# Memory keys as fp32 matmuls, and the input x loaded and normalised earlier, in a hybrid decoder step

## The chip, the cores and the metric

One core of a Trainium2 chip runs the whole program once. The metric is the device time of one execution in microseconds (us); the number to predict is the median of the changed kernel's runs.

## What is computed

One step of a decoder layer for 1024 prompt tokens and 8 sample tokens, 1032 columns together, width 1024. What matters here is its beginning: keys and values of 256 memory tokens, and the norm of x with which every later product starts.

```
def rms_norm(x, g):
    y = xf * rsqrt(mean(xf * xf, axis=-1) + EPS)
    return y * g

def memory_kv(mem, g, w_mk, w_mv):
    m = rms_norm(mem, g)
    k = einsum('bmd,de->bme', m, w_mk)     # 256 x 1024 by 1024 x 1024
    v = einsum('bmd,de->bme', m, w_mv)
...
h = rms_norm(x, g_mix)
z = einsum('btd,de->bte', h, w_in)         # the first product over x: the indexer's keys
```

All arrays are fp32. Behind this come a short convolution, a sparse attention whose keys are picked by an indexer, attention to the memory, a gated feed-forward block and a last norm.

## The kernel before, in words

Everything lies with its features on partitions: x is eight tiles of 128 features by 1032 columns (`xs`), the memory two tiles of 128 by 1024, each with four pieces of 128 features by 256 memory tokens (`memr`). Weights come as units of 128 x 1024 (512 KB), each eight blocks of 128 x 128; `weight_plan` fixes their order. Units 0 to 7 are the memory keys' weights (one for each group of 128 outputs), 8 to 15 the memory values', unit 16 is called "ikdup" (the weight of the indexer's keys, twice side by side), 17 and 18 the indexer's queries, 19 and 20 the attention keys.

To keep fp32 accuracy, a product is made of three matmuls on rounded operands (type fp32r): high by high, high by low, low by high. The high part of a tile is a ScalarE copy to fp32r, the low part the difference to the original, on VectorE or GpSimd. `Weights.split_to` (lines 156 to 169) does that for weights: L164 the high part, L166 the low part, on the engines of `lo_engines` in turn. `take` (L171) loads weights up to `ahead` units further, splits up to `sahead` units and hands out eight blocks. `split_sb` (L491) does it for tiles of x, with the gain folded in when it has a scale (L493, L498).

A hand-made order decides everything: each engine works its instructions in the order of the program text, and the tiles are taken from a ring of 49 slots (`Slots`). All the loads here are issued on SyncE's queue in text order, stores among them being issued at the next `flush`.

At the start (lines 370 to 396) the queue gets the gains, memory and unit 0 in halves, and then units 1 to 8 in turn with the eight tiles of x, then units 9 and 10 and small tensors. Lines 670 to 685 split the memory (scaled by its gain) and unit 0.

The key loop (lines 715 to 747) has eight steps of 24 matmuls of 256 columns (L726). Beside them run the squares of memory (L720), their sums and the row sum (`rstd_sum`, `rstd_chain`, `rstd_rows`: ones-matmuls at L436 and L455, small VectorE steps, copies at L456), squares of x (L697, ScalarE) and their running sum (L703, VectorE), and the evictions (L708), which multiply by the memory's norm. Units 1 to 7 get their low parts on GpSimd and VectorE in turn.

The value loop (lines 758 to 794) has eight steps of 12 matmuls of 512 columns (L770). After step 2 comes the row sum of x's squares, after step 3 the norm's rows (`xR`) and the first two normalisations; `xnorm` (L752, 753) multiplies a tile of x by `xR`, on VectorE for even tiles and on GpSimd for odd ones; from step 4 on a step has one `xnorm` and one `xsplit` (split with the gain); the rest follow the loop. Then `lo_engines` is GpSimd alone.

Next come "ikdup" (`dense`, L809: 72 matmuls of 344 columns at L474, tile k of x wanted by the k-th nine of them), the copies of its result (L503, L506, L812), and `x_sums` (L538), which multiplies two raw tiles of x by the gain on ScalarE (L541) and makes sums and differences of halves on VectorE for the later product units (`unit`, L584, matmuls at L603); it is called four times, in lines 816 to 923. The second attention-key product is copied out by L915, behind the last `x_sums`.

Of the kernel before, what the change touches and what calls it, by code (L numbers as in the profile page):

```python
# [16 lines left out]
T = 1032  # L17
# [13 lines left out]
X_AFTER = (2, 3, 4, 5, 6, 7, 8, 9)  # L31
X_SQUARE = (1, 2, 3, 4, 5, 6, 7, 8)
# [103 lines left out]
class Weights:  # L136
# [19 lines left out]
    def split_to(self, n):  # L156
# [3 lines left out]
        while self.split < n:  # L160
# [8 lines left out]
            self.split += 1  # L169

# [149 lines left out]
def build(tc, A):  # L320
# [56 lines left out]
    def load_x():  # L377
        if len(xs) < 8:
            xs.append(S.get())
            nc.sync.dma_start(xs[-1][0][:, :T], A["xT"][len(xs) - 1])  # L380

    wraw = S.get()
    for hf in range(2):
        c = slice(512 * hf, 512 * hf + 512)
        load_mem(0, hf)
        nc.sync.dma_start(wraw[0][:, c], A["ws"][0][:, c])
    W.loaded = 1
    load_mem(1, 0)
    load_mem(1, 1)
    for n in X_AFTER:  # L390
        W.load_to(n)
        load_x()
# [145 lines left out]
    def x_sums(hl, gi, p, xa, xb):  # L538

        for x, o in ((xa, 2 * p), (xb, 2 * p + 1)):  # L540
            ACT.activation(x[0][:, :T], x[0][:, :T], AF.Copy, scale=gain(gi, o))  # L541
# [128 lines left out]
    mh, ml = [S.get(F32R), S.get(F32R)], [S.get(F32R), S.get(F32R)]  # L670
    msq = [S.get(), S.get()]
    W.lo_engines = [G, V]
    wh, wl = S.get(F32R), S.get(F32R)
    for k in range(8):
        a, c = k // 4, (k % 4) * 256
        ACT.activation(mh[a][0][:, c:c + 256], memr[a][0][:, c:c + 256], AF.Copy, scale=gain(GKV, k))
        V.scalar_tensor_tensor(ml[a][0][:, c:c + 256], memr[a][0][:, c:c + 256], gain(GKV, k),
                               mh[a][0].bitcast(F32)[:, c:c + 256], op0=ALU.mult, op1=ALU.subtract)
        if k in (1, 3):
            c = slice(256 * (k - 1), 256 * (k - 1) + 512)  # L680
            ACT.activation(wh[0][:, c], wraw[0][:, c], AF.Copy)
            V.tensor_tensor(wl[0][:, c], wraw[0][:, c], wh[0].bitcast(F32)[:, c], op=ALU.subtract)
    S.put(wraw)
    W.H[0], W.L[0] = wh, wl
    W.split = 1
# [6 lines left out]
    xR = [None]  # L692
# [21 lines left out]
    dgm = None  # L714
    for j in range(8):
        blocks = W.take(8)
# [17 lines left out]
        if j == 2:  # L734
# [4 lines left out]
        if j == 3:  # L739
            rstd_rows(dgm, 128, mR[0], 256, 256)  # L740
        if j in X_SQUARE:
            x_square(X_SQUARE.index(j))
        if j - 1 in X_SQUARE:
            x_accum(X_SQUARE.index(j - 1))
        if j >= 3:
            for q in ([0, 1, 2, 3] if j == 3 else [j]):
                evict_mk(q)
    S.put(mR)
    dgx = None
    h = []  # L750

    def xnorm(k):  # L752
        (V if k % 2 == 0 else G).tensor_tensor(xs[k][0][:, :T], xs[k][0][:, :T], xR[0][:, :T], op=ALU.mult)

    def xsplit(k):
        h.append(split_sb(xs[k], scale=gain(GMIX, k)))

    for hv in range(2):
        for kp in range(4):
# [14 lines left out]
            j = 8 + step  # L774
            if j in X_SQUARE:
                x_square(X_SQUARE.index(j))
            if j - 1 in X_SQUARE:
                x_accum(X_SQUARE.index(j - 1))
            if step == 2:
                rstd_sum(xacc[0][0], 86, 12)  # L780
                dgx = rstd_chain(86, 12)
                S.put(xacc[0])
                xR = S.get()
            if step == 3:
# [1385 lines left out]
```

## Time and profile before

| what | value |
| --- | --- |
| median of 3 runs | 2087.91 us (2087.48 to 2088.03) |
| time of the profiled execution | 2086.61 us |
| its span in the profile | 2084.8 us |
| busy: TensorE matmuls / weight loads | 2037.8 / 1974.7 us |
| busy: VectorE / ScalarE / GpSimd | 1250.9 / 837.6 / 449.8 us |

The span runs from the first to the last instruction; the time of the execution has some 1.8 us around it. Engines: PE is TensorE's matmul, PEld its weight load, which overlaps PE, DVE is VectorE, ACT ScalarE, POOL GpSimd, SPq SyncE's queue. L166 is line 166 of the kernel. In the chain of waits that ended last, TensorE's two main matmul lines, L603 and L474, stand first with 19% and 15% of the span. Matmuls are pipelined: the recorded duration of one (some 280 ns for 256 columns) is longer than the distance to the next, so rates are read from distances between starts.

### The profile page before, as it was taken

What the parts mean: (1) busy time and instruction counts of PE and PEld (TensorE: products, weight loads), DVE (VectorE), ACT (ScalarE), POOL (GpSimd) and SP (SyncE); (2) the same over time, 40 slices, a digit from 0 to 9 for tenths busy, and PEclk for the clock granted to TensorE, in tenths of its full rate; (3) what the DMA queues carried; (4) which work ended last, traced back from release to release, by engine and by line L of the source; (5) the groups of instructions that cost most, each with busy time, mean ns of one, the idle gap of its engine ahead of it and who ended that gap; (6) DMA issues with size and microseconds to landing.
All of it is one profiled execution on the core that took longest, in us unless ns stands there. A gap on an engine that the chain in (4) does not pass through costs nothing. (4 is left out here: it accounts for less than half of the span.)

```text
span 2084.8 us, 35217 instructions
## 1 busy us (share of the span) xinstructions
PE 2037.8 (98%) x14519; PEld 1974.7 (95%) x14519; DVE 1250.9 (60%) x2169; ACT 837.6 (40%) x1345; POOL 449.8 (22%) x323
## 2 busy tenths in 40 slices
PE   8899999999999999999999999999999999999998
PEld 7799999999999996889999989999999999999997
DVE  7856667788866446861234787467677677721114
ACT  5547767675333334751122252343222222322203
POOL 3410000000000232324424442420000000174404
PEclk9999999999999999999999999999999999999999
DMA  7212221212335531052424424211221321453102
GB/s 295 87 41 82 87 77 62 82 59 65 127 109 214 213 130 54 1 193 92 133 82 152 174 111 163 102 51 58 95 82 62 102 82 62 156 200 102 51 1 82
DMA packets 79874, 217.49 MB, mean 104 GB/s; under 512 B 9690, under 2 KB 24354, under 8 KB 79714
## 3 DMA queue, kind: packets, MB, share of 16 engines
q1 hardware_dynamic: 79170, 214.73, 29.7%
q8 instruction: 113, 1.85, 0.4%
q10 hardware_dynamic: 544, 0.53, 0.1%
q14 instruction: 47, 0.39, 0.1%
HBM read 167.28 MB, written 47.94 MB: 103 GB/s over the span
## 5 line engine op out<-in xcount | busy, mean ns | idle before, releaser
L603 PE MATMUL PS<-t,t 128*128 128x258 f32 x7392 | 894.8, 284 | 7.7 <-DVE t L1893 3.2
L603 PEld LDWEIGHTS PS<-t,t 128*128 128x128 f32 x7392 | 891.6, 190 | 10.8 <-DVE t L1893 3.4
L474 PE MATMUL PS<-t,t 128*128 128x344 f32 x4824 | 770.7, 321 | 2.8 <-POOL t L166 1.2
L474 PEld LDWEIGHTS PS<-t,t 128*128 128x128 f32 x4824 | 762.5, 189 | 6.8 <-POOL t L166 1.8
L166 POOL TENSOR_TENSOR t<-t,t 128x1024 fp32r<-128x1024 f32 x78 | 196.5, 2526 | 415.3 <-ACT t L164 212.1
L246 DVE TENSOR_TENSOR t<-t,t 128x1024 fp32r<-128x1024 f32 (+1 forms) x176 | 188.8, 1086 | 6.4 <-ACT t L233 6.4
L233 ACT ACTIVATE t<-t 128x1024 fp32r<-128x1024 f32 (+1 forms) x176 | 161.6, 946 | 70.6 <-DVE t L223 60.7
L955 ACT ACTIVATE PS<-t,cand 128x1024 f32<-128x1024 f32 (+4 forms) x160 | 143.8, 899 | 54.4 <-DVE cand L962 51.5
L525 POOL TENSOR_TENSOR t<-t,t 128x1032 fp32r<-128x1032 f32 x22 | 53.6, 2453 | 416.6 <-ACT t L524 402.1
L1973 DVE TENSOR_TENSOR t<-PS,t 128x1032 f32<-128x1032 f32 x32 | 39.5, 1233 | 163.0 <-PE PS L474 163.0
L164 ACT ACTIVATE t<-t 128x1024 fp32r<-128x1024 f32 x86 | 89.7, 1050 | 76.0 <-PE PS L474 60.4
L655 DVE TENSOR_TENSOR t<-t,t 128x1032 f32<-128x1032 f32 (+1 forms) x100 | 114.1, 1149 | 2.8 <-ACT t L1879 2.3
L609 DVE TENSOR_TENSOR t<-PS,t 128x516 f32<-128x516 f32 x44 | 30.6, 695 | 109.2 <-PE PS L603 109.2
L607 ACT COPY t<-PS 128x516 f32<-128x516 f32 x44 | 25.9, 588 | 166.4 <-PE PS L603 166.1
L1534 DVE TENSOR_TENSOR t<-PS,t 128x1032 f32<-128x1032 f32 x32 | 39.4, 1232 | 79.9 <-PE PS L474 79.9
L1605 DVE CUSTOM_DVE_ANT_0 caus<-t,t 128x256 bf16<-128x256 f32 x128 | 79.0, 617 | 10.0 <-ACT t L1647 5.2
L493 ACT ACTIVATE t<-t 128x1032 fp32r<-128x1032 f32 (+2 forms) x24 | 25.5, 1068 | 132.9 <-DVE t L1517 76.9
L496 POOL TENSOR_TENSOR t<-t,t 128x1032 fp32r<-128x1032 f32 (+1 forms) x22 | 53.5, 2438 | 109.1 <-ACT t L493 91.3
L1094 POOL COPY co<-cst 128x8 f32<-128x8 f32 x8 | 1.5, 192 | 340.4 <-DVE cst L1089 340.4
L1226 POOL TENSOR_SCALAR t<-t,ast 128x128 f32<-128x128 f32 (+7 forms) x64 | 47.8, 747 | 120.4 <-DVE ast L1225 84.6
L612 ACT COPY t<-PS 128x516 f32<-128x516 f32 x26 | 15.3, 590 | 144.8 <-PE PS L603 144.8
L524 ACT ACTIVATE t<-t 128x1032 fp32r<-128x1032 f32 x40 | 41.4, 1059 | 74.9 <-PE PS L474 44.9
(272 smaller groups left out, 2108.6 us busy)
## 6 DMA issues: line engine op xcount, KB each, us to landing
t<-in_ws_dram SPq DMA_DIRECT2D x86, 512.0 KB, 5.2
t<-in_wu_dram SPq DMA_DIRECT2D x44, 512.0 KB, 4.3
t<-in_wu_dram SPq DMA_DIRECT2D x88, 256.0 KB, 5.5
fd<-t SPq DMA_DIRECT2D x18, 516.0 KB
t<-fd SPq DMA_DIRECT2D x18, 516.0 KB, 10.1
t<-in_xT_dram SPq DMA_DIRECT2D x16, 516.0 KB, 7.1
t<-in_cmk_dram SPq DMA_DIRECT2D x16, 512.0 KB, 5.9
t<-in_cmv_dram SPq DMA_DIRECT2D x16, 512.0 KB, 5.4
```

Of the source, the lines that this page charges most:

```text
L164: nc.scalar.activation(h[0][:, :1024], raw[0][:, :1024], AF.Copy)
L166: eng.tensor_tensor(l[0][:, :1024], raw[0][:, :1024], h[0].bitcast(F32)[:, :1024], op=ALU.subtract)
L233: self.nc.scalar.activation(h[0][:, :w], self.raw[u][x][0][:, :w], AF.Copy)
L246: self.nc.vector.tensor_tensor(l[0][:, o:o + w], raw[0][:, :w], h[0].bitcast(F32)[:, :w], op=ALU.subtract)
L474: PE.matmul(PS[:, b + c, :CH], w, x[0][:, c * CH:(c + 1) * CH], start=(k == 0 and p == 0), stop=(k == n - 1 and p == 2))
L496: (lo or G).tensor_tensor(l[0][:, :width], src[0][:, :width], hf, op=ALU.subtract)
L525: lo.tensor_tensor(l[0][:, a:b], raw[0][:, a:b], h[0].bitcast(F32)[:, a:b], op=ALU.subtract)
L603: PE.matmul(PS[:, banks[z] + c, :HC], a, b[:, HC * c:HC * c + HC], start=j < 3 and q == 0 and p == 0 or j == 5 and q == 0 and p == 0, stop ...
L655: V.tensor_tensor(o, o, i, op=ALU.mult)
L955: ACT.activation(wide[:, :128 * (i + 1)], sc[i], AF.Sign, bias=candf[:, n:n + 1], scale=-1.0, accum_out=tval[:, n:n + 1])
L1226: G.tensor_scalar(p, p, a[:, 3:4], 1.0, op0=ALU.mult, op1=ALU.mult)
L1605: V.tensor_tensor_reduce(out=caus, in0=s[0][:, 256 * x:256 * x + 256], in1=rows, scale=1.0, scalar=0.0, op0=ALU.mult, op1=ALU.add, accum_o ...
```

## The change

The memory keys are computed with one fp32 matmul for each block in place of three fp32r matmuls. Their weights are used as loaded (`take_raw`), without a split; the memory, multiplied by its gain, is one tile pair `mg`, made by ScalarE and VectorE in turn, and is split only at step 2, for the values. x is loaded two tiles at a time between units 2 and 6, squared in steps 1 to 5 of the keys, and its row sums come behind step 6, its norm's rows behind step 7. In the value loop each step has one `xnorm`, now with the gain in it and on VectorE, and one `xsplit` with its low part on VectorE. Since x then holds the gain, `x_sums` leaves out its ScalarE passes in its four calls. The weights' low parts are on VectorE up to unit 20, and on GpSimd again from `begin_conv_out` on.

```
-X_AFTER = (2, 3, 4, 5, 6, 7, 8, 9)
-X_SQUARE = (1, 2, 3, 4, 5, 6, 7, 8)
+X_SQUARE = {1: (0,), 2: (1,), 3: (2, 3), 4: (4, 5), 5: (6, 7)}
...
+    def take_raw(self):
+
+        self.load_to(self.cur + 1 + self.ahead)
+        self.cur += 1
+        return self.raw.pop(self.cur - 1)
+
...
-    W.loaded = 1
+        nc.sync.dma_start(w0[0][:, c], A["ws"][0][:, c])
+    W.loaded, W.split = 1, 8
     load_mem(1, 0)
     load_mem(1, 1)
-    for n in X_AFTER:
-        W.load_to(n)
-        load_x()
+    for w, x in ((3, 2), (4, 4), (5, 6), (6, 8)):
+        W.load_to(w)
+        load_x(x)
     W.load_to(11)
...
-        for x, o in ((xa, 2 * p), (xb, 2 * p + 1)):
-            ACT.activation(x[0][:, :T], x[0][:, :T], AF.Copy, scale=gain(gi, o))
+        if gi is not None:
+            for x, o in ((xa, 2 * p), (xb, 2 * p + 1)):
+                ACT.activation(x[0][:, :T], x[0][:, :T], AF.Copy, scale=gain(gi, o))
...
-    W.lo_engines = [G, V]
-    wh, wl = S.get(F32R), S.get(F32R)
+    mg = [S.get(), S.get()]
+    W.lo_engines = [V]
     for k in range(8):
         a, c = k // 4, (k % 4) * 256
...
+        o, i = mg[a][0][:, c:c + 256], memr[a][0][:, c:c + 256]
+        if k % 2 == 0:
+            ACT.activation(o, i, AF.Copy, scale=gain(GKV, k))
+        else:
+            V.tensor_scalar(o, i, gain(GKV, k), None, op0=ALU.mult)
...
+    def xnorm(k):
+        V.scalar_tensor_tensor(xs[k][0][:, :T], xs[k][0][:, :T], gain(GMIX, k), xR[0][:, :T], op0=ALU.mult, op1=ALU.mult)
+
+    def xsplit(k):
+        h.append(split_sb(xs[k], lo=V))
+
     for j in range(8):
-        blocks = W.take(8)
+        w = W.take_raw()
         flush()
...
-        order = [(p, k) for k in range(8) for p in range(3)] if j == 0 else [(p, k) for p in range(3) for k in range(8)]
-        for p, k in order:
+        for k in range(8):
             a, c = k // 4, (k % 4) * 256
-            w, x = ((0, mh), (0, ml), (1, mh))[p]
-            PE.matmul(PS[:, j % 6, :256], blocks[k][w], x[a][0][:, c:c + 256], start=(k == 0 and p == 0),
-                      stop=(k == 7 and p == 2))
-        W.close()
+            PE.matmul(PS[:, j % 6, :256], w[0][:, 128 * k:128 * k + 128], mg[a][0][:, c:c + 256], start=k == 0, stop=k == 7)
+        S.put(w)
...
-        if j == 2:
+        if j == 1:
             rstd_sum(msq[0][0], 128, 2)
...
-        if j == 3:
+        if j == 2:
             rstd_rows(dgm, 128, mR[0], 256, 256)
...
+            for a in range(2):
+                hl = split_sb(mg[a], lo=V, width=1024)
+                mh.append(hl[0])
+                ml.append(hl[1])
+        for k in X_SQUARE.get(j, ()):
+            x_square(k)
+        for k in X_SQUARE.get(j - 1, ()):
+            x_accum(k)
+        if j >= 2:
+            for q in ([0, 1, 2] if j == 2 else [j]):
                 evict_mk(q)
+        if j == 6:
+            rstd_sum(xacc[0][0], 86, 12)
+            dgx = rstd_chain(86, 12)
+            S.put(xacc[0])
+            xR = S.get()
+            W.split_to(9)
+        if j == 7:
+            rstd_rows(dgx, 86, xR[0], T, CH)
...
             step = 4 * hv + kp
...
+            xnorm(step)
+            if step >= 1:
+                xsplit(step - 1)
...
-    W.lo_engines = [G]
-    for k in range(4, 8):
-        if k < 6:
-            xnorm(k + 2)
-        xsplit(k)
+    xsplit(7)
...
     def begin_conv_out():
+        W.lo_engines = [G]
```

## Rows read from the trace of the kernel before

**Rows 1.** The page, part 1: busy time, share of span, instructions of each engine

```profile
PE 2037.8 (98%) x14519; PEld 1974.7 (95%) x14519; DVE 1250.9 (60%) x2169; ACT 837.6 (40%) x1345; POOL 449.8 (22%) x323
```

**Rows 2.** Busy time by stretches: width, PE, PEld, DVE, ACT, POOL, granted clock, DMA

```profile
6.00:11.00 5.00, 4.62 (x17) 3.99 (x18) 4.02 (x9) 3.74 (x9) 0.00 (x0) 1.00 0.96 365
...
63.00:70.00 7.00, 0.00 (x0) 0.00 (x0) 7.00 (x3) 0.65 (x1) 7.00 (x3) 0.72 0.04 17
70.00:76.00 6.00, 5.81 (x18) 5.43 (x19) 6.00 (x5) 3.47 (x4) 2.39 (x1) 0.50 0.24 90
```

**Rows 3.** Waits of PE from 0 to 190 us: total, times, longest

```profile
PE PS L770 <- DVE t L166: 8.2, 2, 7.5
...
PE PS L603 <- ACT t L915: 2.5, 1, 2.5
...
PE PS L474 <- POOL t L166: 1.0, 1, 1.0
```

**Rows 4.** Groups by line and shape, 46 to 72 us: busy, mean ns, idle before

```profile
L753 POOL TENSOR_TENSOR t<-t,t 128x1032 f32<-128x1032 f32 x4 | 13.6, 3411 | 0.8 <-ACT t L793 0.8
...
L166 DVE TENSOR_TENSOR t<-t,t 128x1024 fp32r<-128x1024 f32 x2 | 6.8, 3414 | 0.0
```

**Rows 5.** Timeline of DVE and ACT, 40 to 86 us: start, duration of the group

```profile
40.70 2.56 DVE L703 TENSOR_TENSOR t<-t,t 128x1032 f32<-128x1032 f32 x2
...
42.02 1.23 DVE L703 TENSOR_TENSOR t<-t,t 128x1032 f32<-128x1032 f32 x1
...
73.40 2.49 DVE L498 SCALAR_TENSOR_TENSOR t<-t,gains,t 128x1032 fp32r<-128x1032 f32 x2
75.81 1.22 DVE L753 TENSOR_TENSOR t<-t,t 128x1032 f32<-128x1032 f32 x1
...
85.64 1.03 ACT L503 ACTIVATE t<-PS 128x1032 fp32r<-128x1032 f32 x1 [5.42 <-PE PS L474]
```

**Rows 6.** Timeline of PE: fp32r streams of 256, 512 and 344 columns

```profile
28.88 7.17 PE L726 MATMUL PS<-t,t 128*128 128x256 f32 x56 [1.81 <-DVE t L166]
35.89 8.92 PE L770 MATMUL PS<-t,t 128*128 128x512 f32 x36
...
163.22 11.55 PE L474 MATMUL PS<-t,t 128*128 128x344 f32 x72
```

**Rows 7.** Timeline of PE and PEld around fp32 matmuls, L1037 and L2030

```profile
618.42 3.65 PE L1037 MATMUL PS<-t,t 64*32 64x257 f32 x16
...
622.00 0.22 PE L1038 MATMUL PS<-iwc,sel 8*32 8x4 f32 x2
...
2051.79 0.19 PEld L1993 LDWEIGHTS PS<-t,t 128*128 128x128 f32 x1 [0.17 <-issue]
2052.15 0.98 PEld L1993 LDWEIGHTS PS<-t,t 128*128 128x128 f32 x6 [0.17 <-issue]
```

**Rows 8.** Groups of PE, 6.3 to 11 and 12 to 16 us; timeline, first instructions

```profile
L726 PE MATMUL PS<-t,t 128*128 128x256 f32 x17 | 4.9, 456 | 3.9 <-ACT t L681 3.9
...
L726 PE MATMUL PS<-t,t 128*128 128x256 f32 x37 | 4.5, 280 | 0.0
...
6.38 10.56 PE L726 MATMUL PS<-t,t 128*128 128x256 f32 x64 [3.90 <-ACT t L681]
...
10.61 1.06 ACT L164 ACTIVATE t<-t 128x1024 fp32r<-128x1024 f32 x1 [0.16 <-DMA t<-in_ws_dram]
...
15.75 1.06 ACT L164 ACTIVATE t<-t 128x1024 fp32r<-128x1024 f32 x1 [0.28 <-DMA t<-in_ws_dram]
```

**Rows 9.** Timeline: row sums of x's squares, rows of the norm, VectorE's last copy

```profile
44.65 1.93 PE L436 MATMUL PS<-ones,t 128*86 128x1 f32 x24
...
49.31 2.20 PE L455 MATMUL PS<-t,ones 86*128 86x344 f32 x6
...
51.55 0.52 DVE L456 COPY t<-PS 128x344 f32<-128x344 f32 x1 [0.94 <-PE PS L455]
```

**Rows 10.** Timeline: the low part of unit 18 on POOL

```profile
96.10 2.68 POOL L166 TENSOR_TENSOR t<-t,t 128x1024 fp32r<-128x1024 f32 x1 [13.21 <-ACT t L164]
```

More of the change, by code (lines that the diff above doesn't have):

```diff
@@ L375, in load_mem, with load_x @@
         nc.sync.dma_start(memr[a][0][:, c], A["memT"][:, 4 * a + 2 * hf:4 * a + 2 * hf + 2, :].rearrange("p k m -> p (k m)"))
-    def load_x():
-        if len(xs) < 8:
+    def load_x(n):
+        while len(xs) < n:
             xs.append(S.get())
             nc.sync.dma_start(xs[-1][0][:, :T], A["xT"][len(xs) - 1])
-    wraw = S.get()
+    w0 = S.get()
+    W.raw[0] = w0
     for hf in range(2):
@@ L385, in build @@
         load_mem(0, hf)
-        nc.sync.dma_start(wraw[0][:, c], A["ws"][0][:, c])
-    W.loaded = 1
+        nc.sync.dma_start(w0[0][:, c], A["ws"][0][:, c])
+    W.loaded, W.split = 1, 8
     load_mem(1, 0)
     load_mem(1, 1)
-    for n in X_AFTER:
-        W.load_to(n)
-        load_x()
+    for w, x in ((3, 2), (4, 4), (5, 6), (6, 8)):
+        W.load_to(w)
+        load_x(x)
     W.load_to(11)
@@ L668, in join @@
         return out
-    mh, ml = [S.get(F32R), S.get(F32R)], [S.get(F32R), S.get(F32R)]
     msq = [S.get(), S.get()]
-    W.lo_engines = [G, V]
-    wh, wl = S.get(F32R), S.get(F32R)
+    mg = [S.get(), S.get()]
+    W.lo_engines = [V]
     for k in range(8):
         a, c = k // 4, (k % 4) * 256
[L676 to L685, printed above, removed]
+        o, i = mg[a][0][:, c:c + 256], memr[a][0][:, c:c + 256]
[3 more added lines that the diff above has]
+            V.tensor_scalar(o, i, gain(GKV, k), None, op0=ALU.mult)
     mR = S.get()
@@ L691, in build @@
     xacc = [None]
-    xR = [None]
     xsq = [None] * 8
@@ L712, in evict_mk @@
                   mstage[a][0][:, :1024].rearrange("p (k m) -> p k m", m=256), mstage[a])
-    dgm = None
+    dgm = dgx = None
+    mh, ml = [], []
+    h = []
+    def xnorm(k):
+        V.scalar_tensor_tensor(xs[k][0][:, :T], xs[k][0][:, :T], gain(GMIX, k), xR[0][:, :T], op0=ALU.mult, op1=ALU.mult)
+    def xsplit(k):
+        h.append(split_sb(xs[k], lo=V))
     for j in range(8):
-        blocks = W.take(8)
+        w = W.take_raw()
         flush()
@@ L738, in build @@
             S.put(msq[0])
-        if j == 3:
+        if j == 2:
             rstd_rows(dgm, 128, mR[0], 256, 256)
[L741 to L746, printed above, removed]
-                evict_mk(q)
-    S.put(mR)
[L749 to L756, printed above, removed]
+            for a in range(2):
[8 more added lines that the diff above has]
+            for q in ([0, 1, 2] if j == 2 else [j]):
+                evict_mk(q)
+        if j == 6:
[6 more added lines that the diff above has]
+            rstd_rows(dgx, 86, xR[0], T, CH)
+    for t in mg:
+        S.put(t)
+    S.put(mR)
     for hv in range(2):
@@ L773, in build @@
             step = 4 * hv + kp
[L774 to L784, printed above, removed]
-                rstd_rows(dgx, 86, xR[0], T, CH)
-                xnorm(0)
-                xnorm(1)
-            if step >= 4:
-                xnorm(step - 2)
-                xsplit(step - 4)
+            xnorm(step)
+            if step >= 1:
+                xsplit(step - 1)
         for m in range(2):
@@ L815, in build @@
     store(A["o_ikT"], iks[0][0:64, :T], iks)
-    x_sums(h, GMIX, 0, xs[0], xs[1])
+    x_sums(h, None, 0, xs[0], xs[1])
     iqs = const.tile([64, NS, 4], F32, name="iqs")
@@ L831, in build @@
         if jt == 0:
-            x_sums(h, GMIX, 1, xs[2], xs[3])
+            x_sums(h, None, 1, xs[2], xs[3])
     vnew = const.tile([NS, 256], F32, name="vnew")
@@ L922, in build @@
             for p in (2, 3):
-                x_sums(h, GMIX, p, xs[2 * p], xs[2 * p + 1])
+                x_sums(h, None, p, xs[2 * p], xs[2 * p + 1])
             UW.high(0, "V")
```

## The prediction

> **What bounds the kernel now.** I read the page's table of engines first: TensorE has work for 98% of the span and VectorE for 60% [rows 1], so a change pays only by taking TensorE's idle, slow or superfluous time away. The busy time by stretches shows where that is, in the first 86 us, where most of the change lies: between 63 and 70 us TensorE does nothing while VectorE and GpSimd are busy throughout, and from 70 to 76 its granted clock is 0.50 [rows 2]. The engine's waits name the causes [rows 3]: 8.2 us at the memory-value matmuls for VectorE's low part of a weight (line 166), 1.0 us later for one from GpSimd, and 2.5 us at the first product units for a ScalarE copy (L915). The groups of 46 to 72 us show why VectorE is late: its low parts of weights, 128x1024, take 3.4 us there, as GpSimd's normalisations beside them do [rows 4]. Where GpSimd is silent, two such passes take 2.41 us (73.40 to 75.81), 1.20 each, and the two slowest that I found start 1.32 apart (40.70 and 42.02) [rows 5]. So the stretch is bound by two element-wise engines that slow each other. The output of "ikdup", the first matrix product over x, reaches ScalarE at 85.64 [rows 5]; I follow that moment.
>
> The sum is made on the profiled execution: span 2084.8, its time 2086.61. The median of the three runs, 2087.91, is 1.3 higher, so I subtract the gain from 2087.9. About 0.2% (4.2 us) is what a measurement of this kernel can tell from no change.
>
> **Part 1: fp32 keys on TensorE.** Removed are 24 matmuls for each of 8 steps, at (35.89 - 28.88) / 56 = 0.125 us each, 3.0 us a step [rows 6]. Added are 8 fp32 matmuls of 256 columns a step. The program records one fp32 matmul as two instructions. The nearest stream is L1037: 16 instructions, thus 8 fp32 matmuls of 257 columns, from 618.42 to 622.00, where L1038 follows, 0.4475 us each [rows 7]. Its stationary tiles are only 32 wide, so I look at a 128-wide one too: around L2030 (430 columns) the weight loads behind it start at 2051.79 and 2052.15, 0.36 us apart, which is 2 x 430 columns at 2.4 GHz: the loads were hidden [rows 7]. So a step costs 8 x 0.4475 = 3.58 us. Bounds: 4 x 256 columns at 2.4 GHz, 0.427 each (3.41 a step), and a load wholly in the open, 0.19 us (the load at 2051.79) before each of the 16 instructions, 3.0 us more a step [rows 7]. I take 3.58, the row of a stream of nearly this width.
>
> A rule of the Trainium skill speaks against the hidden load: "TensorE: Matmul & The Clock Gate", section "What overlaps and what doesn't", says that a weight load overlaps matmuls in flight only when it goes to other row groups. The same page of the Trainium skill, section "LDWEIGHTS (loading the stationary operand)", gives columns / 1.2 ns, 107 ns for 128; an estimate from it makes the sum 12 us longer (112 loads at full clock), 2091.7 us. The fp32r stream at 0.125 us for 256 columns, of which 0.107 are streaming, disagrees with it.
>
> **Part 2: the start.** The first step may begin when half of W0 and the scaled memory are there, near 5.8 us: before, it began at 6.38, held by a ScalarE pass over half of W0 (L681), which is gone and is about half of L164's 1.06 [rows 8]. The mean matmul of 6.3 to 11 us takes 456 ns against 280 from 12 to 16 [rows 8], so I read half clock there, 1.2 GHz, although the stretch is given as 1.00 [rows 2]. I take the rise at 11.4, between those two rows, as before: six and a half fp32 matmuls at 4 x 256 / 1.2 GHz = 0.853, the rest at 0.4475, and some tenths of waiting for memory: the first step ends at 12.2. Bound below 11.0 (full clock), above 13.9 (the rise comes late). Weight 1 landed at 10.61 and weight 3, four transfers behind it, at 15.75 [rows 8]: 1.29 us a transfer. In the new order weights 3 to 6 stand at places 5, 8, 11 and 14: they land at 15.8, 19.6, 23.5 and 27.3. The steps want them at 20, 24, 28 and 31, so loading x earlier costs nothing: the slower keys cover it. Without that cover it would be two transfers, 2.6 us. The last x, place 13, lands at 26.0; its square and sum follow during steps 5 and 6.
>
> **Part 3: keys to values.** 12.2 + 7 x 3.58 = 37.3; the two small reductions of the memory's norm 0.8 (4 instructions at 1.93 / 24 and one fp32 matmul at 0.45); the 12 row sums of x, now before the last step, 1.9 [rows 9]: the keys end at 40.0, against 35.9 before [rows 6]. The rows of x's norm take 2.1 us more of TensorE and VectorE's last copy of them ends 2.76 us after the first matmul of the three (49.31 to 52.07) [rows 9]: values begin at 42.1, VectorE is free for x at 42.7. Until then its work is about 22 us of 40 by count (four scalings, three sums and two low parts of memory, 7 sums of x, 8 evictions, chains), hidden under the matmuls. The splits that go (2 x 8 pieces of memory in two parts, weights 0 to 7 with 8 high and 8 low parts) cost nothing now to anything late.
>
> **Part 4: values and x.** TensorE: 96 matmuls at (44.65 - 35.89) / 36 = 0.243, 23.4 us [rows 6, 9], so ikdup could start at 65.5. VectorE now does for each of 8 steps a low part of weight, one normalisation with gain, one low part of x. Ikdup's weight (W16) stands behind 8 low parts of weights, 7 normalisations and 6 low parts of x, 21 passes. At 1.20 [rows 5] that is 25.2 us: 67.9. The bounds are 1.32 and TensorE's own pace, by which nothing waits. Each value step wants a low part only for its last third, so the steps wait at most some tenths. Ikdup does six matmuls and waits 1.4 us, from about 66.5 to 67.9. The rest is 66 matmuls at 11.55 / 72 = 0.160 [rows 6], 10.6, and 0.2 to reach ScalarE: 78.7 instead of 85.6. Gain **6.9 us**. The last low part of x is done at 71.5, before ikdup wants it at 77. In the idle stretch of before the clock fell only on the way (0.72 on average from 63 to 70, with half and full as its levels) [rows 2], some 3 us in; 1.4 us is less, so I expect no slow stretch. By my count about 40 of the 49 slots are in use at most, so no load waits for one.
>
> **Part 5: behind it.** The low parts of W17 to W20 move from GpSimd to VectorE. W18 came off GpSimd at 96.10 + 2.68 = 98.78 and TensorE waited 1.0 for it [rows 3, 10]; on VectorE, two us earlier, it doesn't: gain **1.0**. The four passes cost 1.2 each beside VectorE's gaps in the scores. Eight ScalarE passes (L541) go; the 2.5 us for L915 [rows 3] stay but for a tenth, because that copy stands behind ScalarE passes that VectorE's sums release: gain **0.25**, bounds 0 and 2.5. Later work is TensorE's own and keeps what was gained.
>
> Sum: 6.9 + 1.0 + 0.25 = 8.2, rounded; time 2087.9 - 8.2 = **2079.7 us**.
>
> **Rivals.** *A, slower:* the fp32 weight load is not hidden. The stationary operand changes with each instruction, and a 190 ns load stands before each of 112 instructions: 21.3 us, and all behind follows the keys, so 2101.0. It decides from 8.2 / 112 = 73 ns of open load. For it: fp32 loads of 128 columns are few in the trace. Against: the starts in rows 7. Chance 0.08. The rule of the Trainium skill above is this rival at a smaller price.
>
> *B, no change that can be told:* VectorE's chain becomes the wait that replaces the old one. If its passes follow at 1.32 us, W16 is ready at 70.4, TensorE stands idle 3.9 us, and the clock falls as it did in 63 to 70 us [rows 2]: 2.5 us more, and half of the 6 us at 0.50, 3.0. Time 2085.2. For: VectorE has 3.6 us a step, TensorE 2.9. Against: nothing is left on GpSimd to slow it. Chance 0.16.
>
> *C, no change:* ikdup is earlier, but a later stage, a transfer or a search step released by VectorE, takes it back: 2087.9. Against: 98% of the span is TensorE work. Chance 0.06. That the change doesn't do what it says would show as three matmuls per pair in keys; the new loop issues one, so no chance is kept for it.
>
> **Numbers.** The forecast has 0.70. Its own bounds: fp32 at 0.427 gives 1.1 less, an early clock 1.2, no wait for VectorE 1.4: 2076.0. Fp32 at 0.467 (twice the stream's surplus over 0.427) gives 1.1 more, a late clock 1.7, passes at 1.24 0.8: 2083.3. To leave out no more than 2 in 10 the range reaches past B: 2076 to 2086.5. A and C lie outside. Faster by over 0.2%: 0.70; within: B and C, 0.22; slower: 0.08.
>
> **What would show it.** Right: key steps 3.5 to 3.6 us apart; no GpSimd pass from 10 to 110 us; VectorE passes at 1.2 us; ikdup's output on ScalarE at 77 to 80; full clock from 60 to 90; no wait at the second weight of the indexer queries. Wrong: weight loads in line with the fp32 matmuls, key steps over 4.2 us, a wait for weights or x in the keys, or half clock at ikdup.

## The result and the profile after

The changed kernel takes 2075.52 us (median of 5 runs, 2075.18 to 2076.43). The kernel before took 2087.48 in the same comparison (5 runs, 2086.69 to 2088.03). The ratio is 0.9942, with a 95% interval of 0.9931 to 0.9952: faster by 0.6%. The profiled execution took 2075.18, its span is 2073.4, and its mean granted clock is 0.997 (before: 2086.61, 2084.8, 0.995).

The first part of the page, to be held against [rows 1]:

```profile
span 2073.4 us, 35037 instructions
...
PE 2037.3 (98%) x14455; PEld 1972.7 (95%) x14455; DVE 1236.9 (60%) x2174; ACT 821.6 (40%) x1326; POOL 402.5 (19%) x307
```

TensorE's busy time is the same as before to half a microsecond (2037.8): its work in the keys became longer, and matmuls that had run at half clock became shorter. The 11.4 us that the span lost are therefore, by these sums, almost all idle time of TensorE. Where it was idle, the busy time by stretches shows (columns as in [rows 2]; the last row is for later):

```profile
63.00:70.00 7.00, 5.66 (x33) 5.20 (x34) 7.00 (x7) 4.24 (x5) 0.00 (x0) 1.00 0.33 128
70.00:76.00 6.00, 6.00 (x40) 6.00 (x39) 0.98 (x1) 0.00 (x0) 0.00 (x0) 1.00 0.00 0
...
1440.00:1800.00 360.00, 360.00 (x2995) 360.00 (x2994) 260.17 (x308) 97.20 (x117) 7.50 (x3) 1.00 0.24 80
```

From 63 to 70 us TensorE had done nothing and now works for 5.66 us; GpSimd (the column with 0.00) was busy throughout and is now silent; VectorE has seven passes there, in whole or in part, not three. From 70 to 76 the granted clock is 1.00 and no longer 0.50. TensorE's waits from 0 to 190 us, against [rows 3]:

```profile
PE PS L733 <- DMA t<-in_ws_dram: 3.1, 1, 3.1
PE PS L610 <- ACT t L908: 2.2, 1, 2.2
...
PE PS L480 <- DVE t L165: 1.3, 1, 1.3
...
PE PS L781 <- DVE t L165: 0.3, 1, 0.3
```

The 8.2 us at the memory values are now 0.3 (L781), the wait of 1.0 for GpSimd is gone, the wait for the ScalarE copy (now L908) is 2.2 instead of 2.5, and a wait of 1.3 at ikdup is new. TensorE's timeline (start, duration of the group), against [rows 6, 9]; L733 is the key matmul, x16 is one step:

```profile
5.60 10.10 PE L733 MATMUL PS<-t,t 128*128 128x256 f32 x32 [3.12 <-DMA t<-in_ws_dram]
15.53 0.50 PE L442 MATMUL PS<-ones,t 128*128 128x1 f32 x4
...
19.86 13.98 PE L733 MATMUL PS<-t,t 128*128 128x256 f32 x64
33.68 1.93 PE L442 MATMUL PS<-ones,t 128*86 128x1 f32 x24
...
39.01 2.20 PE L461 MATMUL PS<-t,ones 86*128 86x344 f32 x6
40.78 19.42 PE L781 MATMUL PS<-t,t 128*128 128x512 f32 x82
...
169.90 2.31 PE L610 MATMUL PS<-t,t 128*128 128x258 f32 x17 [2.16 <-ACT t L908]
```

Four key steps take 33.68 - 19.86 = 13.82 us, 3.455 each, 0.432 for one fp32 matmul. The keys end at 39.0, 3.1 later than before, and the values begin at 40.78, 4.9 later. VectorE and ScalarE, against [rows 5]:

```profile
41.24 0.52 DVE L462 COPY t<-PS 128x344 f32<-128x344 f32 x1 [0.94 <-PE PS L461]
41.80 1.23 DVE L165 TENSOR_TENSOR t<-t,t 128x1024 fp32r<-128x1024 f32 x1
42.94 1.29 DVE L719 SCALAR_TENSOR_TENSOR t<-t,gains,t 128x1032 f32<-128x1032 f32 x1
44.15 1.22 DVE L165 TENSOR_TENSOR t<-t,t 128x1024 fp32r<-128x1024 f32 x1
...
65.05 1.21 DVE L165 TENSOR_TENSOR t<-t,t 128x1024 fp32r<-128x1024 f32 x1
...
69.76 1.22 DVE L165 TENSOR_TENSOR t<-t,t 128x1024 fp32r<-128x1024 f32 x1
...
86.53 1.22 DVE L165 TENSOR_TENSOR t<-t,t 128x1024 fp32r<-128x1024 f32 x1
```

```profile
77.12 1.03 ACT L509 ACTIVATE t<-PS 128x1032 fp32r<-128x1032 f32 x1 [7.59 <-PE PS L480]
```

From 41.80 to 66.26, the end of ikdup's low part, lie 21 passes without a gap, 1.165 us each. Ikdup's output is on ScalarE at 77.12 instead of 85.64. So a stage that starts 4.9 us later ends 8.5 us earlier: it is 13.4 us shorter. Of these, 3.6 are only work moved ahead of it (the row sums and norm rows of x), 6.6 are waits of TensorE (8.2 before, 0.3 and 1.3 after), and the rest, some 3, are the half clock that came behind the long wait (70 to 76 us). The groups of 46 to 72 us say why, against [rows 4] (count, then busy, mean ns of one):

```profile
L502 DVE TENSOR_TENSOR t<-t,t 128x1032 fp32r<-128x1032 f32 x8 | 9.8, 1225 | 0.0
L719 DVE SCALAR_TENSOR_TENSOR t<-t,gains,t 128x1032 f32<-128x1032 f32 x7 | 9.0, 1285 | 0.0
L165 DVE TENSOR_TENSOR t<-t,t 128x1024 fp32r<-128x1024 f32 x7 | 8.5, 1216 | 0.0
```

The low part that took 3414 ns takes 1216. VectorE alone does 22 passes here, where before each of the two engines did 7 (VectorE was free for them from 52.1 us). How the gain builds up along the two profiled executions:

| moment | before | after | gain |
|---|---|---|---|
| ikdup's output reaches ScalarE | 85.64 | 77.12 | 8.5 |
| first attention value matmul | 109.33 | 99.51 | 9.8 |
| product units go on behind the ScalarE copy | 180.17 | 169.90 | 10.3 |
| last ScalarE copy L570 of before (L577 after) | 1415.0 | 1404.8 | 10.2 |
| last VectorE add L617 of before (L624 after) | 1813.4 | 1802.4 | 11.0 |
| end of the span | 2084.8 | 2073.4 | 11.4 |

### The profile page after: what moved, and what is told of

It reads as the page before. It is cut to its first block, busy times and chain, and to the rows that moved or that the text cites. A ratio compares the mean times of both kernels' runs of the same rounds, so it can differ in the third digit from the quotient of the medians.

```text
span 2073.4 us, 35037 instructions
## 1 busy us (share of the span) xinstructions
PE 2037.3 (98%) x14455; PEld 1972.7 (95%) x14455; DVE 1236.9 (60%) x2174; ACT 821.6 (40%) x1326; POOL 402.5 (19%) x307
## 5 line engine op out<-in xcount | busy, mean ns | idle before, releaser
L610 PEld LDWEIGHTS PS<-t,t 128*128 128x128 f32 x7392 | 890.8, 189 | 10.2 <-DVE t L1887 3.4
L165 POOL TENSOR_TENSOR t<-t,t 128x1024 fp32r<-128x1024 f32 x66 | 160.8, 2446 | 354.9 <-ACT t L163 326.5
L163 ACT ACTIVATE t<-t 128x1024 fp32r<-128x1024 f32 x79 | 82.3, 1051 | 72.8 <-PE PS L480 60.9
L499 ACT ACTIVATE t<-t 128x1032 fp32r<-128x1032 f32 (+2 forms) x34 | 36.0, 1067 | 142.2 <-DVE t L1511 77.1
L1599 DVE CUSTOM_DVE_ANT_0 caus<-t,t 128x256 bf16<-128x256 f32 x128 | 78.7, 615 | 10.3 <-ACT t L1641 5.3
L1239 DVE TENSOR_TENSOR t<-PS,t 128x512 fp32r<-128x512 f32 x72 | 49.6, 688 | 32.1 <-ACT t L1235 31.4
```

What stands on the lines that cost most here:

```text
L163: nc.scalar.activation(h[0][:, :1024], raw[0][:, :1024], AF.Copy)
L165: eng.tensor_tensor(l[0][:, :1024], raw[0][:, :1024], h[0].bitcast(F32)[:, :1024], op=ALU.subtract)
L610: PE.matmul(PS[:, banks[z] + c, :HC], a, b[:, HC * c:HC * c + HC], start=j < 3 and q == 0 and p == 0 or j == 5 and q == 0 and p == 0, stop ...
L1239: V.tensor_tensor(tl[0][:, :512], PS[:, t_bank(x), :], th[0].bitcast(F32)[:, :512], op=ALU.subtract)
L1599: V.tensor_tensor_reduce(out=caus, in0=s[0][:, 256 * x:256 * x + 256], in1=rows, scale=1.0, scalar=0.0, op0=ALU.mult, op1=ALU.add, accum_o ...
```

## The experiments

Theory 1: the gain is GpSimd's passes beside VectorE, which are gone; fp32 keys, the early norm and the order of the loads bring nothing at ikdup by themselves. The rivals give it to these. Every kernel was timed 5 to 11 times. Its whole time turned out a blunt tool: executions of one kernel differ by up to 5 us (2076.51 to 2081.57 with the loads in turn), and half-clock stretches come at places that the change does not touch (the section on surprises). So each kernel is judged first at two moments that lie ahead of most of them, ikdup's output and the first attention value matmul (times in us from the profiles; medians and ratios, each to the kernel before in the same comparison, from all the runs).

| kernel | ikdup's output | first value matmul | median | ratio to before, 95% interval |
|---|---|---|---|---|
| before | 85.6 | 109.3 | 2087.1 to 2088.0 | 1 |
| after | 77.1 | 99.5 | 2075.52 | 0.9942 (0.9931 to 0.9952) |
| after, again | 76.5 | 98.9 | 2077.03 | 0.9950 (0.9936 to 0.9963) |
| before without the GpSimd passes | 77.6 | 100.0 | 2079.00 | 0.9959 (0.9945 to 0.9972) |
| after, engines shared as before | 83.0 | 106.8 | 2085.23 | 0.9987 (0.9978 to 0.9996) |
| after, four low parts on GpSimd | 77.8 | 100.2 | 2079.25 | 0.9960 (0.9947 to 0.9974) |
| before with fp32 keys alone | 86.7 | 110.4 | 2094.21 | 1.0028 (1.0017 to 1.0038) |
| after with three-pass keys | 85.1 | 107.5 | 2091.13 | 1.0016 (1.0007 to 1.0025) |
| after, norm late | 77.2 | 99.6 | 2082.00 | 0.9974 (0.9964 to 0.9983) |
| after, loads in turn | 77.3 | 99.6 | 2080.07 | 0.9962 (0.9949 to 0.9976) |
| after, later low parts on GpSimd | 76.5 | 98.9 | 2077.90 | 0.9954 (0.9940 to 0.9967) |
| after, gain on ScalarE | 77.1 | 99.7 | 2077.23 | 0.9951 (0.9938 to 0.9965) |
| after, W16 first | 75.5 | 97.9 | 2074.64 | 0.9940 (0.9926 to 0.9953) |
| W16 first and sums moved | 75.5 | 97.9 | 2076.81 | 0.9949 (0.9936 to 0.9963) |

**The changed kernel once more**, with no edit, for the scatter between sessions and to see which of the 11.4 us come back.

> The changed kernel once more, nothing edited. If what the profile gained behind 1400 us (0.75 us spread evenly over the product units, 0.5 us in the last 15 us) is chance, this profile's distances to that of the first run of the same kernel scatter by several tenths there and its median lies within 0.7 us of 2075.5. If it is an effect of the change, this profile shows the same 0.75 and 0.5 against the kernel before: the output of ikdup on ScalarE at 77.1, the last product unit 11.0 earlier than before, span within 0.2 of 2073.4.

Measured: a median of 2077.03, 1.5 above the first one where at most 0.7 had been expected, and a span of 2075.1. Ikdup's output came 0.6 earlier, as did the start of the values (40.2): the first key steps ran faster. The 0.8 us that the first table gains between 1415 and 1813 us come from the pace: from 1440 to 1800 us, all at a granted clock of 1.00 and without idle time, this is the row of the kernel before

```profile
1440.00:1800.00 360.00, 360.00 (x2989) 360.00 (x2989) 259.61 (x312) 96.56 (x116) 5.05 (x2) 1.00 0.23 74
```

with 2989 matmuls against 2995 after, in both executions: 0.2%, 0.7 us. By the test above that would be an effect of the change. But kernels derived from before show either pace (2994 with fp32 keys alone, 2989 without the GpSimd passes), and those derived from after lie between 2992 and 2995, so it goes with no single part of the change. What sets the pace is not shown, and this part of the 11.4 is not counted as the change's.

**Before without the GpSimd passes.** The keys, the loads and the late norm stay as they were; besides the passes, the gain moves into the normalisation and the sums of x lose their ScalarE passes (a kernel below shows that this gives nothing at ikdup).

```
+        if j == 7:
+            W.lo_engines = [V]
         blocks = W.take(8)
...
-        (V if k % 2 == 0 else G).tensor_tensor(xs[k]..., xs[k]..., xR...)
+        V.scalar_tensor_tensor(xs[k]..., xs[k]..., gain(GMIX, k), xR...)
...
-        h.append(split_sb(xs[k], scale=gain(GMIX, k)))
+        h.append(split_sb(xs[k], lo=V))
...
-    W.lo_engines = [G]
```

> The kernel before with one thing taken over from the change: no GpSimd pass from weight 8 to weight 20 (low parts and normalisations on VectorE, gain in the normalisation, no ScalarE passes in the sums of x). Keys stay three fp32r matmuls with their splits on GpSimd and VectorE, x's loads, squares and norm stay where they were. Theory 1 (VectorE without GpSimd beside it is the gain, keys and early x are not): as in the run with the norm late, x's chain starts at 52, 20 passes of 1.17, ikdup's output at 77 to 79 and the first product units 8 to 10 us earlier than before, median 2076 to 2081. Rival (fp32 keys are needed as well): ikdup's output at 82 to 86, median 2083 to 2088.

The groups of 46 to 72 us and the waits of TensorE in this kernel:

```profile
L755 DVE SCALAR_TENSOR_TENSOR t<-t,gains,t 128x1032 f32<-128x1032 f32 x8 | 10.2, 1290 | 0.1
...
L166 DVE TENSOR_TENSOR t<-t,t 128x1024 fp32r<-128x1024 f32 x5 | 6.1, 1219 | 0.0
```

```profile
PE PS L474 <- DVE t L166: 1.3, 1, 1.3
PE PS L772 <- DVE t L166: 0.8, 2, 0.4
```

The 8.2 us at the value matmuls shrank to 0.8, and ikdup's output came at 77.6: 8.1 of the 8.5 us, without fp32 keys, early norm or new order of loads, as Theory 1 expected. This settles the main cause at ikdup. By medians it is 8.1 us, against 12.0 for the change in its first comparison and 10.9 in its second; its profiled execution, 2076.76, is 1.6 above after's. The last passes here start at 72.11 to 75.54, later than after (69.76), because the norm is in the way; TensorE loses little by that: the new wait of 1.3 at ikdup (L474) is as long as after's.

**The other way round:** after, with GpSimd taking every second low part and normalisation again, and the gain back on ScalarE.

```
+            W.lo_engines = [G, V]
             W.split_to(9)
...
-        V.scalar_tensor_tensor(xs[k]..., gain(GMIX, k), xR...)
+        (V if k % 2 == 0 else G).tensor_tensor(xs[k]..., xR...)
```

> The changed kernel with the engines of before from the values on: low parts of weights 8 to 16 on GpSimd and VectorE in turn, 17 to 20 on GpSimd, odd normalisations on GpSimd without gain, the gain in the split and again in the sums of x. The norm still comes before the values. Theory 1: 9 GpSimd passes in the values each cost VectorE 2.2 us (as four did in the run with weights alone), VectorE's chain is 16 x 1.17 + 9 x 2.2 = 38.5 us from 41.8, ikdup's output at 81 to 84, and 1.0 more is lost at weight 18: median 2081 to 2085. Theory 2: the early norm keeps the gain, ikdup's output at 77 to 78.5, median 2076.5 to 2079.

The groups of 46 to 72 us:

```profile
L504 DVE SCALAR_TENSOR_TENSOR t<-t,gains,t 128x1032 fp32r<-128x1032 f32 x6 | 19.2, 3219 | 1.2 <-ACT t L499 1.2
...
L165 POOL TENSOR_TENSOR t<-t,t 128x1024 fp32r<-128x1024 f32 x3 | 10.2, 3416 | 6.6 <-ACT t L163 6.6
L719 POOL TENSOR_TENSOR t<-t,t 128x1032 f32<-128x1032 f32 x3 | 10.2, 3406 | 0.0
```

The passes of 3.2 to 3.4 us are back on both engines, TensorE waits 4.9 us at the values (two waits, 2.5 the longest), and ikdup's output moves from 77.1 to 83.0: 5.9 of the 8.5 us are given back with fp32 keys, early norm and load order all kept, as Theory 1 expected (its median, 2085.23, is 0.2 above Theory 1's range). The other 2.6 us are what these are worth while GpSimd still shares the passes; without its passes they are worth only the 0.4 of the run above.

**The price of one GpSimd pass:** four low parts of weights back on GpSimd, all else on VectorE.

```
+            W.lo_engines = [G, V]
             W.split_to(9)
...
+    W.lo_engines = [V]
     xsplit(7)
```

> The changed kernel with the low parts of weights 8 to 16 on GpSimd and VectorE in turn, as the kernel before had them. Theory 1 (the two engines slow each other): GpSimd passes of 3.4 us, VectorE passes beside them of 3.4 instead of 1.2; VectorE loses some 8 us and saves 4 passes (4.7), TensorE waits in the last value steps, ikdup's output at 80 to 82 instead of 77.1, median 2079 to 2080. Rival (work shared is work gained): VectorE's chain is 5 passes shorter, the waits of 0.3 and 1.3 us for its low parts go, ikdup's output at 75.5, median 2074.

The timeline of GpSimd and, below, of VectorE:

```profile
56.52 2.42 POOL L165 TENSOR_TENSOR t<-t,t 128x1024 fp32r<-128x1024 f32 x1 [4.41 <-ACT t L163]
64.56 2.40 POOL L165 TENSOR_TENSOR t<-t,t 128x1024 fp32r<-128x1024 f32 x1 [5.62 <-ACT t L163]
```

```profile
56.60 3.42 DVE L719 SCALAR_TENSOR_TENSOR t<-t,gains,t 128x1032 f32<-128x1032 f32 x1
...
64.57 3.47 DVE L719 SCALAR_TENSOR_TENSOR t<-t,gains,t 128x1032 f32<-128x1032 f32 x1
...
72.67 1.22 DVE L165 TENSOR_TENSOR t<-t,t 128x1024 fp32r<-128x1024 f32 x1
```

This is the clearest picture of the mechanism. GpSimd's pass runs from 56.52 to 58.94; VectorE's, which starts 0.08 later, ends at 60.02, 1.08 behind GpSimd's end. Alone it takes 1.28, so it got through at most 0.2 us of its work beside GpSimd: it stood still for nearly the whole of GpSimd's pass. Each of the four cost VectorE 2.2 us and saved it 1.2. From the first pass to the last one shown VectorE's chain is 72.67 - 40.55 = 32.1 us long, after 69.76 - 41.80 = 28.0: 4.1 longer, four times 1.0. TensorE lost only 0.7 at ikdup, and about 1.9 counted from the start of the values, which were 1.25 earlier here (39.53): ikdup's own low part was on GpSimd and early (its wait is 0.2), and 2.9 us of waits at the value matmuls came in its place. Both theories missed ikdup's output. The median, 2079.25, lies in Theory 1's range, but by luck, since most of what Theory 1 put into it is not there at ikdup.

**fp32 keys alone:** before, with the raw weights in the keys and nothing else changed.

```
-        blocks = W.take(8)
+        w = W.take_raw()
...
+        for k in range(8):
+            PE.matmul(PS[:, j % 6, :256], w[0][:, 128 * k:128 * k + 128], mg[a][0][:, c:c + 256], start=k == 0, stop=k == 7)
```

> The kernel before with fp32 keys alone: weights 0 to 7 unsplit, memory scaled first and split at step 2, everything about x as before. Theory 1 (the fp32 matmuls cost TensorE time and only make room for the rest): keys end at 37 to 38 instead of 35.9, the value stage waits as before, ikdup's output at 86 to 88 against 85.6, median 2088 to 2090. Rival (the keys themselves are the gain: fewer splits, fewer waits): ikdup's output at 77 to 80, median 2076 to 2080.

```profile
PE PS L777 <- DVE t L166: 8.2, 2, 7.6
```

That row of the waits of TensorE shows the old 8.2 us untouched. The values begin at 37.5 (before 35.9), and ikdup's output is 1.1 later. That is Theory 1. The median is 6.3 above before; the profile has three more half-clock stretches than that of before, all behind ikdup, so the whole 6.3 is not the price of the keys.

**Three fp32r passes in the keys**, with the rest of the change kept (weights 0 to 7 split on GpSimd and VectorE as before):

```
-        w = W.take_raw()
+        if j == 7:
+            W.lo_engines = [V]
+        blocks = W.take(8)
```

> The changed kernel with the keys of before: three fp32r matmuls, weights 0 to 7 split on ScalarE, GpSimd and VectorE in turn, memory split at the start; x loaded, squared, normalised as in the change, no GpSimd pass from weight 8 on. Theory 1 (x early and VectorE alone in the values are the gain): keys end between 36 and 40 (VectorE is nearly full there), ikdup's output at 75 to 79, median 2074 to 2078. Rival (without fp32 keys nothing is gained): VectorE is overloaded in the keys, x's sums come 8 us late, ikdup's output at 84 or later, median 2084 to 2088.

```profile
PE PS L441 <- DVE t L708: 4.4, 1, 4.4
...
PE PS L441 <- DVE t L747: 2.7, 1, 2.7
```

L441 is the row sums of squares. With the splits of eight weights, the squares of x and the norm ahead of the values, VectorE has too much in the keys, TensorE waits 7.1 us there, and the granted clock is 0.50 from 40 to 46 us. The values begin at 48.8; from there the stage is as quick as after. Ikdup's output, 85.1, is the rival's number (84 or later), and Theory 1's missed: fp32 keys are worth nothing on the path by themselves, but they are what makes room for the early norm.

**Is the early norm needed?** After, with x's row sums behind value step 2 and the norm rows behind step 3; and, in another kernel, the loads of weights and x in turn as before.

```
-        xnorm(step)
-        if step >= 1:
-            xsplit(step - 1)
+        if step == 2:
+            rstd_sum(xacc[0][0], 86, 12)
...
+        if step == 3:
+            rstd_rows(dgx, 86, xR[0], T, CH)
```

> The changed kernel with x's row sums behind value step 2 and the norm's rows behind step 3, as before; everything else of the change stays (fp32 keys, squares of x in the keys, no GpSimd pass). Theory 1 (VectorE freed of GpSimd is the gain): x's chain starts at 52 but has only 20 passes of 1.17 left, ends at 76, ikdup's output at 77 to 79 against 77.1, median within 2 us of the changed kernel. Theory 2 (the norm before the values is the gain): the chain starts 10 us later and so does its end, ikdup's output at 84 to 87, median 2083 to 2088.

```
-    for w, x in ((3, 2), (4, 4), (5, 6), (6, 8)):
-        W.load_to(w)
-        load_x(x)
+    for n in range(2, 10):
+        W.load_to(n)
+        load_x(n - 1)
```

> The changed kernel with weights and tiles of x loaded in turn, as before, so that the last tile of x lands at place 14 instead of 13 and most weights sooner. Theory (the order of the loads decides nothing): keys end, ikdup's output and median as in the changed kernel, within 0.3 us in the profile. Rival (early x is part of the gain): x's sums come late, TensorE waits at the row sums of x, ikdup's output 1 to 3 us later.

Ikdup's output is at 77.2 and 77.3: neither the place of the norm nor the order of the loads decides anything there. Both medians are 4 to 7 us above after all the same, the first beyond its interval, and both expectations of the median missed. In the profile with the late norm three half-clock stretches stand between 1120 and 1420 us; that of after has one there, elsewhere. One of the three by stretches, first this kernel, then after:

```profile
1124.00:1128.00 4.00, 1.12 (x7) 0.64 (x5) 3.96 (x2) 0.00 (x0) 3.88 (x2) 1.00 0.00 0
1129.00:1132.00 3.00, 3.00 (x12) 3.00 (x11) 2.79 (x14) 0.00 (x0) 0.00 (x0) 0.50 0.01 3
```

```profile
1124.00:1128.00 4.00, 3.15 (x21) 2.86 (x20) 2.85 (x2) 0.56 (x2) 4.00 (x2) 1.00 0.01 2
1129.00:1132.00 3.00, 3.00 (x21) 3.00 (x21) 2.79 (x13) 0.00 (x0) 0.00 (x0) 1.00 0.00 0
```

TensorE was idle for 2.9 of 4 us, and behind that twelve matmuls instead of 21 fit into 3 us. What held TensorE is the same collision again. Just ahead, VectorE makes two small copies while GpSimd works through passes of 2.4 us; VectorE's timeline, first with the late norm, then after, and GpSimd's with the late norm:

```profile
1123.17 4.79 DVE L1626 COPY t<-qm_s 128x128 f32<-128x128 f32 x2
```

```profile
1123.35 2.55 DVE L1620 COPY t<-qm_s 128x128 f32<-128x128 f32 x2
```

```profile
1120.76 4.82 POOL L502 TENSOR_TENSOR t<-t,t 128x1032 fp32r<-128x1032 f32 x2 [8.83 <-ACT t L499]
1125.55 2.33 POOL L165 TENSOR_TENSOR t<-t,t 128x1024 fp32r<-128x1024 f32 x1
```

After, the first copy took 0.21 us and only the second was held, for 2.42. With the late norm both were held, 2.49 and 2.38 us, each beside a pass of GpSimd, and TensorE waited for the second. Four of the profiles have both copies held: this one, the loads in turn, fp32 keys alone and the three-pass keys. From 1100 to 1130 us these four lose 3.7 to 5.1 us against after, counted from matmul to matmul, and no other profile loses a tenth. In all fourteen the first copy and GpSimd's next pass start within 0.03 us of each other; in ten the copy gets through first, in four the pass. What decides between them, and why the other half-clock stretches fall where they do, was not settled.

**Part 5's wait at weight 18.** Either the later low parts go back to GpSimd, or the gain goes back to eight ScalarE passes.

```
+    W.lo_engines = [G]
     xsplit(7)
```

> The changed kernel with the low parts of weights 17 to 20 on GpSimd, as before. Theory: TensorE waits 1.0 to 1.3 us at weight 18 again, the attention values begin 1.0 to 1.3 later than in the changed kernel (100.6 instead of 99.5), ikdup's output stays at 77.1 or a few tenths later, as weight 17's pass slows VectorE's last split of x. Median within 0.5 of 1 us above the changed kernel. Rival (GpSimd is quick enough now that ScalarE's gain passes are gone): no wait, no loss.

```
-        V.scalar_tensor_tensor(xs[k]..., gain(GMIX, k), xR..., op0=ALU.mult, op1=ALU.mult)
+        V.tensor_tensor(xs[k]..., xR..., op=ALU.mult)
...
-        h.append(split_sb(xs[k], lo=V))
+        h.append(split_sb(xs[k], scale=gain(GMIX, k)))
```

> The changed kernel with the gain back in the split of x and the eight ScalarE passes back in the sums of x. Expected: ikdup's output at 77.1, no wait at weight 18 (its low part comes 1 us later, still in time), the wait for the second attention-key copy 2.5 instead of 2.2 us: 0.3 lost at the first product units. Rival: the later sums of x bring back a wait at weight 18 of up to 1 us.

Neither brought the wait back: from ikdup's output to the first attention value it is 22.4 and 22.6 us, after 22.4, before 23.7. With both as before (the kernel with the engines shared as before) there is a wait of 1.1 us for GpSimd. So VectorE for the low parts, or no gain passes on ScalarE, is each enough alone to take the wait away, which is a miss wherever it was tied to one of them. With the gain on ScalarE the copy's wait was 2.5 again, as expected.

**A better version?** First, W16's low part ahead of the last normalisations; then also the last sums of x moved behind the second attention key product.

```
             step = 4 * hv + kp
+            if step == 6:
+                W.split_to(W.cur + 2)
             xnorm(step)
```

> The changed kernel with ikdup's weight (16) split in value step 6, ahead of two passes over x. By the chain of VectorE's passes the wait of 1.3 us before ikdup goes and no other comes (the last low part of x is still there 5 us before it is wanted): ikdup's output at 75.8, 1.3 earlier, median 1 to 1.5 below the changed kernel's. Rival (the last low parts of x then hold ikdup): ikdup's output unchanged at 77.

```
-            for p in (2, 3):
-                x_sums(h, None, p, xs[2 * p], xs[2 * p + 1])
-            UW.high(0, "V")
...
+            x_sums(h, None, 2, xs[4], xs[5])
+    x_sums(h, None, 3, xs[6], xs[7])
+    UW.high(0, "V")
```

> As the run before, and the last sums of x and the high and low parts V and W of product unit 0 are put behind the second attention-key product in the text, so that ScalarE's copy of that product (L908, for which TensorE waits 2.2 us) stands ahead of them. Expected: the wait of 2.2 us becomes one of 0 to 0.3 us, first product units 3.4 us earlier than in the changed kernel, median 3 to 3.5 below it. Rival (the sums of x behind it hold the second product instead): gain of the run before and no more.

The first: the wait of 1.3 at ikdup is gone, its output is at 75.5, the median 2074.64 (2073.76 to 2076.75). That beats before beyond the noise (0.9940, 0.9926 to 0.9953), and after by 1.6 us at ikdup with the values beginning at the same 40.8; by medians the two cannot be told apart. The second took the copy's wait of 2.2 away, left two of 0.2 and 0.5, and gained almost nothing, for a new wait took its place on VectorE (its timeline):

```profile
164.29 0.17 DVE L911 COPY ks_new<-t 128x8 f32<-128x8 f32 x1 [2.33 <-ACT t L910]
```

A small copy that needs ScalarE's result now stands ahead of the sums in VectorE's order, and these wait 2.33 us behind it. By the first L624 (L617 of before) the second kernel is 0.4 us ahead of the first (180.5 against 180.9); 2.1 had been expected. Its median, 2076.81, is not below the first's.

## Where the prediction was right, and where it failed

The direction, the mechanism and the order of its terms held; the time came out 4.2 us below the forecast (2087.9 - 12.4 instead of - 8.2) and half a microsecond below the range. What failed is the sizes, in four places. The fp32 matmul of Part 1 was put at 0.4475 us and measured 0.432 (0.9 us over 56 of them). VectorE's pass of Part 4 was put at 1.20 us and measured 1.165 (0.7 us over 21). Part 5 was put at 1.25 us and measured 1.75. And what lies behind the first product units was taken to change nothing ("Later work is TensorE's own and keeps what was gained"), and so was the distance from profile to median; together they came to 2.2 us, the largest of the four. The range failed with them, as said below. Point by point:

- **Part 1, fp32 keys: the size was off.** I took 0.4475 us a matmul from a stream of 257 columns whose stationary tiles are 32 wide, where 0.432 was measured; 0.427 was my lower bound. The nearest row was nearest in columns and too slow all the same. Over 56 matmuls that is 0.9 us. Rival A is refuted: the weight loads (63 from 20 to 34 us, 190 ns each) lay wholly beside the matmuls, since a step of 3.455 us leaves 0.04 beyond 32 x 256 columns at 2.4 GHz.
- The Trainium skill, "TensorE: Matmul & The Clock Gate", section "What overlaps and what doesn't", would have had these loads, which all go to the same 128 rows, in the open; the measured step of 3.455 us disagrees, here as in the fp32r stream.
- **Part 2, the start: right.** Two steps end at 15.5, the first so at about 12.1 (forecast 12.2). No wait for weights or x followed. Three profiles of this same start (after, after again, four low parts on GpSimd) put the row sums behind the second step at 15.53, 14.93 and 14.28. The moment at which the matmuls reach their full pace, read as the clock's rise, so varies by 1.2 us, as the bounds of 11.0 to 13.9 allowed.
- **Part 3: right, early by Part 1's error.** Keys end at 39.0 (40.0), values begin at 40.78 (42.1), VectorE is free at 41.76 (42.7).
- **Part 4: the mechanism and the count right, the pitch a little off.** W16's low part was the 21st pass, as counted; a pass took 1.165 us on average, not 1.20. I had read 1.20 from a pair of SCALAR_TENSOR_TENSOR passes (L498 at 73.40) and used it for all. After, the seven normalisations of that form still take 1.21 from start to start (42.94 to 44.15), but the fourteen low parts are TENSOR_TENSOR passes and take 1.13 to 1.15 (41.80 to 42.94): 0.7 us over 21. Ikdup waited 1.34 us (1.4), the clock stayed at 1.00, and the output came at 77.12 (78.7). Rival B is refuted by the pitch (it needed 1.32) and the clock.
- Why GpSimd's passes cost so much was only read off as "two engines slow each other". The kernel with four low parts on GpSimd shows one pass of VectorE waiting for nearly the whole of one of GpSimd's. The 3.4 us of both engines in [rows 4] can then be read as 2.2 + 1.2, each waiting for the other in turn. The Trainium skill, "SBUF — State Buffer", section "Who interferes with whom", states this: a VectorE instruction with two inputs in SBUF contends with a GpSimd instruction that reads SBUF. The trace agrees, with 3.42 us against 1.28 for the same VectorE pass.
- **Part 5: right in sign, the reason too narrow.** From ikdup to the attention values 1.3 us went (forecast 1.0), up to the product units another 0.45 (0.25). I put the first down to W18's low part being on VectorE. Two runs show that it is not needed: with ScalarE's eight gain passes gone GpSimd is in time as well. Which of the shorter queues gives the 0.3 beyond the wait itself was not separated.
- **Rival C did not come true after:** of the 10.3 us behind the ScalarE copy 10.2 are left at 1415 us and 11.4 at the end. It was not idle, though: the second profile of the same kernel had gained 10.9 us there and 9.8 at the end, and four kernels of the experiments lost 3.7 to 5.1 us around 1123 us.
- **What the sum had no term for.** The 4.2 us are 1.6 at ikdup (0.9 and 0.7 above), 0.5 in Part 5, 0.7 of pace from 1415 to 1813 us, 0.5 at the very end, and 1.0 between profiled execution and median (1.3 before, 0.3 after). No run ties the last three, 2.2 us, to the change: at the very end, the clock fell to half beside the last pair of norm rows before (1.23 us, at 2076.62) and just behind it after (0.70 us, at 2065.66).
- **The range.** Its lower end added up bounds of Parts 1, 2 and 4, 3.7 us below the forecast; each of these was met. It had no term for the two executions, and it left out the bound that Part 5 itself gives, 2.5 us where the sum has 0.25. With that it would have begun at 2073.8. That the miss is small is chance: the same kernel's second median, 2077.03, lies inside the range.

What stays open: why kernels whose first 180 us are alike meet one to three half-clock stretches between there and the last 20 us, why two small copies are held in some of them and one in others, what sets the pace from 1440 to 1800 us, and the 0.3 us named above.

## What to carry to other kernels

Before two element-wise engines share passes, look in the trace at what a pass of each takes while the other runs. If one stands still for the whole of the other's, offloading a pass costs the first engine more (2.2 us here) than doing it itself (1.2). A matmul that costs TensorE more (fp32 keys, 3 us) can be worth it for the element-wise work that it spares, but only if that work is on the path; alone it lost 1.1 us at ikdup. Judge an edit worth a few microseconds at a moment just behind it, and give the whole time a range for the execution itself. Then look through the rest of the trace all the same: a collision a thousand microseconds behind the edit cost four of these kernels 3.7 to 5.1 us, about a third of the whole gain or more.

## What the hardware showed beyond expectation

- A VectorE pass that started with a GpSimd pass took 3.42 to 3.47 us and ended 1.08 behind it; alone it takes 1.2 to 1.3. I had read only that the two slow each other, not that one stands still. A copy of 128x128, which took 0.21 us when it was not held, took 2.42 beside a GpSimd pass of 2.46.
- The granted clock falls to 0.50 for some microseconds in mid-kernel, at one to six places of a profile that differ between kernels and, by the scatter of their times, probably between executions. Where it was looked at above, TensorE had been idle for 2.9 us just before, and three microseconds then held 12 matmuls instead of 21. Behind the same wait of 2.16 us for ScalarE's copy the clock fell to 0.50 in one execution of the changed kernel (the second, from 170.3 us, 1.5 us lost) and not in the other.
- One execution ran 0.2% slower than another over 360 us of unbroken matmuls, both with a granted clock of 1.00 (2989 and 2995 matmuls).
- Fp32 matmuls of 256 columns with a new 128x128 stationary tile for each of their two instructions stream at 0.432 us, 1% above 4 x 256 columns at 2.4 GHz.
